# Pads at both ends of on-chip memory, dense operands at multiples of 512 bytes, and stored weight parts for one output chunk only

## The chip, the cores and the metric

One core of one Trainium2 chip. The metric is device time in microseconds (us), the median over runs of the whole program. Times of the kernel before: 3194.85, 3198.68 and 3200.09 us.

## What is computed

One hybrid decoder layer in fp32 on x of 1024 tokens by 2048 channels: a layer norm with shift and scale from a conditioning vector, one wide input projection, two mixers side by side (native sparse attention and a diagonal state-space layer with a GLU), their gated sum, an output projection and a second norm. Cut to what bears on the change:

```python
h = _ln(x) * (1.0 + scale[:, None, :]) + shift[:, None, :]
proj = h @ w_in[i]
...
m = jax.nn.sigmoid(ga) * (o_a @ w_branch_nsa[i]) + jax.nn.sigmoid(gb) * (o_b @ w_branch_ssm[i])
y = m @ w_out[i]
x = _ln(DEEPNORM_ALPHA * x + gate[:, None, :] * y) * ln_g[i] + ln_b[i]
```

All dense products run on TensorE with fp32 split into two parts: a value is cast to fp32r (`hi`), the rest is `lo`, and a product is hi·hi + hi·lo + lo·hi, three matmuls of 128x128 (stationary) by 128x512 (moving).

## The kernel before

The program is written in a tile framework: tiles come from pools, and a scheduler orders each engine's instructions by a priority (the program's order, with weight units raised by `WPRI`). All DMAs are issued by SyncE (SP) on one queue, in order.

**Input products** (`mm6`, L126, L127, L130). `w_unit` (L106) loads 128x512 of weights (`wraw`, L111), casts them on ScalarE (`whi`, L113) and takes the rest on VectorE (`wlo`, L115). The weights are the stationary operand, the normed input (`hhi`, `hlo`, 32 tiles in the pool `xh` on the right side of on-chip memory) is the moving one.

**Branch products** (`product`, L487 to L489). Weights are stationary again; the moving operand is `op`, from the pool `opd` on the left side or `opx` on the right (the second half of the tokens in `glu` and `branch_ssm`).

**Output projection** (`out_tokens`, L601; `times`, L617, matmuls L619 to L621). Here the roles are swapped: `m`, the merged branches, is stationary (pool `mp`, right side), and weights are moving. It runs twice, first for the tokens 512 to 1023, then (`final`) for 0 to 511. Each run goes over four chunks `c` of 512 output columns, each of 16 k's and 4 blocks of 128 tokens. In the first run the weights of chunks 0 and 3 are stored after the split, as parts, in DRAM (`wo_d`, stores at L633); the second run loads these parts (`wohi`, `wolo`, L628) instead of loading, casting and subtracting again. Chunks 1 and 2 are split anew in both runs. During chunk 3 of the first run the `m` of the second half is loaded (`mraw`, L558) and split (L560, L561). During chunk 0 of the second run the norms of the first run (`later`) are done: L611 on ScalarE, L612 and L613 on VectorE, stores to `out` at L614. In chunk 3 of the second run (`split_up`) the four blocks go in two pairs, and the parts of k = 8 to 15 are loaded ahead (`kept`) into `opd`; they are used after k = 0 to 7.

**Where the operands lie.** Left-hand pools are stacked upwards from the end of the constants' pool `cst`, right-hand pools downwards from the top. All dense tiles are multiples of 512 bytes per partition, so one offset holds for a whole side: in the built kernel before, the left pools begin at 416 modulo 512, the right ones at 480. Moving/stationary offsets are thus 480/416 for the input products, 416/416 for branch products with `opd` (480/416 with `opx`), and 416/480 for the output projection.

Of the kernel before, what the change touches and what calls it, by code (L numbers as in the profile page):

```python
# [5 lines left out]
F32 = mybir.dt.float32  # L6
# [11 lines left out]
KT = 16  # L18
# [7 lines left out]
PS_, PT, PWB, WR = 3, 2, 4, 2  # L26
MR = 2
EARLY = (6, 6, 6, 4)


def hybrid_kernel(tc, A, out):
# [19 lines left out]
def _hybrid(es, tc, A, out):  # L51
# [31 lines left out]
    bf_d = scratch("bf_d", [128, 512])  # L83
    ob_d = [[scratch(f"ob_d{hf}_{i}", [2, 128, 512]) for i in range(8)] for hf in range(2)]
    oa_d = [[scratch(f"oa_d{hf}_{g}", [2, 128, 2, 512]) for g in range(G)] for hf in range(2)]
    wo_d = {c: [[scratch(f"wo_d{c}_{k}_{i}", [128, 512]) for i in range(2)] for k in range(KT)] for c in (0, 3)}
    mb_d = [scratch(f"mb_d{i}", [128, 512]) for i in range(16)]

    cst = es.enter_context(tc.tile_pool(name="cst", bufs=1))
    ident = cst.tile([128, 128], F32, name="ident")  # L90
    ld(ident, A["ident"])
    ones = cst.tile([128, 128], F32, name="ones")
    V.memset(ones, 1.0)
    bada = cst.tile([128, KT, 2], F32, name="bada")
    ld(bada, A["bada"])
    mods = cst.tile([128, KT, 2], F32, name="mods")
    gts = cst.tile([128, NB, 48], F32, name="gts")

    wp = es.enter_context(tc.tile_pool(name="wp", bufs=3))
    stp = es.enter_context(tc.tile_pool(name="st", bufs=3))  # L100

# [43 lines left out]

    NS = 3
    units = []


    def load_wa(n):  # L150
# [204 lines left out]
    def gate_steps():  # L355

        for c in range(4):
            gp = bank()
            for hf in range(2):
                cs = slice(512 * c + 256 * hf, 512 * c + 256 * hf + 256)  # L360
                o = gp[:, 256 * hf:256 * hf + 256]
                for u in range(4):
                    wg = stp.tile([128, 4, 256], F32, name="wg", tag="stg")
                    ld(wg, A["w_gate"][4 * u:4 * u + 4, :, cs].rearrange("k p c -> p k c"))
                    for i in range(4):
                        r = 32 * i
                        PE.matmul(o[r:r + 32], cP[:, 4 * u + i], wg[:, i], start=u == 0, stop=u == 3, tile_position=(0, r))
                    yield
            cs = slice(512 * c, 512 * c + 512)
            s = stage()  # L370
            t, b = s[:, :512], s[0:32, 512:]
            S.copy(t, gp)
            S.copy(b, gp[0:32])
            ld(b, A["b_gate"][0:1, cs].to_broadcast([32, 512]))
            g2 = bank()
            PE.matmul(g2[0:32], ones[:, 0:32], t, start=True, stop=True)
            V.tensor_tensor(b, b, g2[0:32], op=ADD)
            st_(gate_d[:, cs], b[0:1])

# [80 lines left out]
    p1.close()  # L460


    hb = cst.tile([128, 8], F32, name="hb")
    ld(hb, A["b_glu"])
    V.tensor_scalar(hb, hb, 0.5, None, op0=MUL)

# [134 lines left out]
    def out_tokens(m, hf, final, ahead=None, later=iter(())):  # L601

        r, stt = [None] * 4, [None] * 4

        def norm(b, n=2):
            mv = row_stats(nc, tl, stt[b])
            nm = tl.tile([128, 1], F32, name="nm", tag="nm", bufs=2)
            V.tensor_scalar(nm, mv[:, 0:1], mv[:, 1:2], -1.0, op0=MUL, op1=MUL)
            for c in range(n):
                cs = slice(D // n * c, D // n * (c + 1))  # L610
                S.activation(r[b][:, cs], r[b][:, cs], AF.Identity, bias=nm, scale=mv[:, 1:2])  # L611
                V.tensor_tensor(r[b][:, cs], r[b][:, cs], rows["ln_g"][:, cs], op=MUL)  # L612
                V.tensor_tensor(r[b][:, cs], r[b][:, cs], rows["ln_b"][:, cs], op=ADD)  # L613
                ld(out[512 * hf + 128 * b:512 * hf + 128 * b + 128, cs], r[b][:, cs])  # L614
                yield

        def times(a, mk, b, hi, lo, k):  # L617
            t = slice(128 * b, 128 * b + 128)
            PE.matmul(a, mk[0][:, t], hi, start=k == 0, stop=False)  # L619
            PE.matmul(a, mk[0][:, t], lo, start=False, stop=False)  # L620
            PE.matmul(a, mk[1][:, t], hi, start=False, stop=k == KT - 1)  # L621

        def parts(c, k, pool=None):

            if final and c in wo_d:
                hl = [(pool or wp).tile([128, 512], F32R, name="wo" + n, tag="op" if pool else "w" + n) for n in ("hi", "lo")]
                for t, d in zip(hl, wo_d[c][k]):
                    rd(f(t), d)  # L628
            else:
                hl = w_unit(A["w_out"][k][:, 512 * c:512 * c + 512], [128, 512], tl)  # L630
                if c in wo_d:
                    for t, d in zip(hl, wo_d[c][k]):
                        st_(d, f(t))  # L633
            return hl

        for c in range(4):
            cs = slice(512 * c, 512 * c + 512)
            split_up = final and c == 3
            if ahead and c == 3:
                ahead()  # L640
            kept = {}
            if split_up:

                with tc.high_priority(offset=WPRI):
                    kept = {k: parts(c, k, opd) for k in range(8, KT)}
            for bs in ((0, 1), (2, 3)) if split_up else (range(4),):
                acc = [psum_a() if c % 2 and b > 1 else psum_e() for b in bs]
                for k in range(8 if split_up else KT):
                    with tc.high_priority(offset=WPRI):
                        hi, lo = parts(c, k)  # L650
                    for b, a in zip(bs, acc):
                        times(a, m[k], b, hi, lo, k)
                    if c == 0:
                        next(later, None)
                for b, a in zip(bs, acc):
                    for k in kept:
                        times(a, m[k], b, *kept[k], k)
                    x = fetch(A["x"][512 * hf + 128 * b:512 * hf + 128 * b + 128, cs])[:, :512]
                    S.mul(x, x, ALPHA)
                    if c == 0:  # L660
                        r[b] = tl.tile([128, D], F32, name="r", tag="r", bufs=5)
                        stt[b] = tl.tile([128, 4, 6], F32, name="stt", tag="stt", bufs=5)
                    with tc.high_priority(offset=WPRI if split_up else 0):
                        V.tensor_tensor(r[b][:, cs], a, rows["gate"][:, cs], op=MUL)
                        V.tensor_tensor(r[b][:, cs], r[b][:, cs], x, op=ADD)
                        V.bn_stats(stt[b][:, c], r[b][:, cs])
                    if split_up:
                        for _ in norm(b, 4 if b == 3 else 2):
                            pass
        return (None for b in range(4) for _ in norm(b, 4))  # L670
# [97 lines left out]
class Attention:  # L768
# [25 lines left out]
    def group(self, g):  # L794
        V, rd, NK = self.nc.vector, self.rd, self.NK
        self.g = g

        def f(ap):
            return ap.bitcast(F32)


        if self.first == 0:
            self.window_keys(0, NK)
        self.KS = self.tl("ks", [128, NK], F32R, "k")
        rd(f(self.KS), self.k_d[0][g].rearrange("i d t -> (i d) t")[:, :NK])

        self.BN = self.tl("bn", [128, 4, 256], F32, "kv")
        t = self.tz_d[g]
        rd(self.BN, bass.AP(tensor=t.tensor, offset=t.offset + 127, ap=[[383, 128], [384 * 128, 4], [1, 256]]))

        self.VC = self.tl("vc", [128, 2, 128], F32R, "kv")
        for e in range(2):
            V.memset(f(self.VC)[64 - 64 * e:128 - 64 * e, e], 0.0)
            rd(f(self.VC)[64 * e:64 * e + 64, e], self.vcc_d[:, g])
        if self.BF is None:
            self.BF = self.tl("bf", [128, 384])
            t = self.bf_d
            rd(self.BF, bass.AP(tensor=t.tensor, offset=t.offset + 127, ap=[[511, 128], [1, 384]]))
        nb = NK // 128
        self.VS = self.tl("vs", [128, nb, 128], F32R, "kv")  # L820
        self.VW = self.tl("vw", [128, nb, 128], F32R, "kv")
        for v, t in ((self.VW, self.v_d[1][g]), (self.VS, self.v_d[0][g])):
            for hf in range(2):
                c = slice(4 * hf, min(4 * hf + 4, nb))
                rd(f(v)[:, c], t[hf][:, :c.stop - c.start])
        self.BC = self.tl("bc", [128, 4, 120 - 8 * self.first], F32, "kv")
        V.memset(self.BC[:, :, 0:48], 0.0)
        V.memset(self.BC[:, :, 63:], NEG)
        V.tensor_copy(self.BC[:, :, 48:63], self.BN[:, :, 31:256:16])

    def window_keys(self, key0, n):

# [17 lines left out]
    def unit(self, qb):  # L850
# [37 lines left out]
        joint = key0 == 0  # L888

        def compressed(h, ps):  # L890
            b0 = 56 - 8 * qb
            m = reduce(0, h, [(ps, self.BC[:, h, b0:b0 + 64], pc[:, h])])
            S.activation(pc[:, h], pc[:, h], AF.Exp, bias=m, scale=-1.0, accum_out=sums[:, h, 0:1])

# [574 lines left out]
```

## Time and profile before

| | |
|---|---|
| runs, us | 3194.85, 3198.68, 3200.09 |
| profiled execution, us | 3197.64 |
| its span, us | 3195.9 |
| mean granted TensorE clock (share of 2.4 GHz) | 0.992 |
| TensorE busy | 97% of the span, 15573 instructions |
| VectorE, ScalarE busy | 51%, 35% |
| moved by DMA | 459.38 MB, mean 144 GB/s |

The profile is one execution. Busy shares say which engine is full over the whole span; windows of it say which one is full in a stretch. A matmul's time in the rows runs from its start to its last result; consecutive matmuls overlap, so the distance from start to start is shorter than that.

### The profile page before, as it was taken

The numbers are of one execution on the slowest core, as the hardware profiler recorded it, in microseconds if no ns is written. First come the engines' busy times: TensorE is split into PE (matmuls) and PEld (weight loads), VectorE is DVE, ScalarE is ACT, GpSimd is POOL, SyncE is SP. The second block draws the span as 40 slices with busy tenths as digits, with TensorE's granted clock in tenths as the row PEclk, the third lists the DMA queues.
The fourth block names the chain that finished last, engine by engine and source line by source line (L and its number), as shares of the span: only waits on it lengthen the run. The fifth ranks groups of instructions, "written<-read, shape, count | busy, mean of one in ns | idle before, by whom it ended". The sixth has DMA issues, their size and how long they took to land.

```text
span 3195.9 us, 43129 instructions
## 1 busy us (share of the span) xinstructions
PE 3113.6 (97%) x15573; PEld 2532.1 (79%) x15573; DVE 1632.5 (51%) x4593; ACT 1112.3 (35%) x2313; POOL 34.7 (1%) x36
## 2 busy tenths in 40 slices
PE   7999999999999999999999999999999999999896
PEld 3467788888888888888888888888888887888685
DVE  8445678753443334334433334427877665634535
ACT  4212222222443334333433334325654533323321
POOL 0000000000000000000000000000000000000000
PEclk9999999999999999999999999999999999999999
DMA  9764433344322232222322222246768445756835
GB/s 336 246 180 152 160 110 121 114 130 125 113 90 77 80 104 78 70 70 84 100 78 69 71 86 90 73 158 196 237 197 266 140 131 172 246 194 207 307 115 174
DMA packets 302221, 459.38 MB, mean 144 GB/s; under 512 B 42164, under 2 KB 141812, under 8 KB 302008
## 3 DMA queue, kind: packets, MB, share of 16 engines
q1 hardware_dynamic: 302008, 456.64, 44.7%
q8 instruction: 122, 2.00, 0.3%
q14 instruction: 91, 0.75, 0.1%
HBM read 345.09 MB, written 114.85 MB: 144 GB/s over the span
## 4 chain that ended last, share of the span: by engine, by line
PE 92%; DMA 6%; DVE 1%; SPq 1%; ACT 0%; issue 0%; DVEq 0%; ACTq 0%
PE dps L126 17%; PE dps L130 17%; PE dps L127 17%; PE po L989 4%; PE ps L846 4%; PE pt L967 4%; PE pa L487 3%; PE pa L489 3%; PE pa L488 3%; PE e L619 3%; PE e L620 3%; PE e L621 2%; PE mp L189 1%; DMA wohi<-wo_d 1%; PE pa L619 1%; PE pa L620 1%
## 5 line engine op out<-in xcount | busy, mean ns | idle before, releaser
L126 PE MATMUL dps<-hhi,whi 128*128 128x512 f32 x2336 | 927.3, 397 | 0.0
L127 PE MATMUL dps<-hlo,whi 128*128 128x512 f32 x2336 | 924.2, 396 | 0.0
L130 PE MATMUL dps<-hhi,wlo 128*128 128x512 f32 x2336 | 746.4, 396 | 0.0
L115 DVE TENSOR_TENSOR wlo<-wraw,whi 128x512 fp32r<-128x512 f32 x512 | 353.7, 691 | 632.2 <-ACT whi L113 614.6
L113 ACT CAST whi<-wraw 128x512 fp32r<-128x512 f32 x512 | 316.7, 619 | 997.2 <-PE dps L127 594.2
L126 PEld LDWEIGHTS dps<-hhi,whi 128*128 128x128 f32 x2336 | 440.1, 188 | 101.0 <-issue 9.0
L127 PEld LDWEIGHTS dps<-hlo,whi 128*128 128x128 f32 x2336 | 440.1, 188 | 90.3 <-issue 2.5
L130 PEld LDWEIGHTS dps<-hhi,wlo 128*128 128x128 f32 x2336 | 433.0, 188 | 89.5 <-issue 1.9
L972 DVE TENSOR_TENSOR ptl<-pt,pth 128x512 fp32r<-128x512 f32 (+1 forms) x320 | 196.7, 620 | 270.4 <-ACT pth L971 267.7
L971 ACT CAST pth<-pt 128x512 fp32r<-128x512 f32 (+1 forms) x320 | 166.3, 530 | 441.6 <-PE pt L967 440.3
L487 PE MATMUL pa<-op,whi 128*128 128x512 f32 x528 | 210.2, 400 | 5.5 <-ACT whi L113 3.2
L488 PE MATMUL pa<-op,whi 128*128 128x512 f32 x528 | 209.4, 397 | 2.4 <-DMA op<-oa_d 2.4
L489 PE MATMUL pa<-op,wlo 128*128 128x512 f32 x528 | 209.0, 397 | 0.0
L961 ACT ACTIVATE psl<-psl,mn 128x128 f32<-128x128 f32 (+7 forms) x128 | 99.1, 775 | 89.9 <-DVE mn L874 89.5
L487 PEld LDWEIGHTS pa<-op,whi 128*128 128x128 f32 x528 | 99.9, 189 | 25.8 <-ACT whi L113 4.0
L488 PEld LDWEIGHTS pa<-op,whi 128*128 128x128 f32 x528 | 99.9, 189 | 21.9 <-DMA op<-oa_d 2.8
L489 PEld LDWEIGHTS pa<-op,wlo 128*128 128x128 f32 x528 | 99.8, 189 | 20.0 <-DVE wlo L115 0.4
L620 PE MATMUL e<-wlo,m 128*128 128x512 f32 x288 | 114.4, 397 | 0.0
L621 PE MATMUL e<-whi,m 128*128 128x512 f32 x288 | 113.4, 394 | 0.0
L915 ACT ACTIVATE pw<-pw,mn 128x640 f32<-128x640 f32 (+4 forms) x128 | 88.8, 694 | 29.9 <-DVE mn L874 29.6
L619 PE MATMUL e<-whi,m 128*128 128x512 f32 x288 | 96.4, 396 | 0.0
L846 PE MATMUL ps<-ks,q 128*128 128x512 f32 (+3 forms) x384 | 96.0, 350 | 0.2 <-DVE mn L874 0.2
(306 smaller groups left out, 4223.2 us busy)
## 6 DMA issues: line engine op xcount, KB each, us to landing
wraw<-in_w_in SPq DMA_DIRECT2D x304, 256.0 KB, 3.1
wa<-in_w_ss SPq DMA_DIRECT2D x64, 512.0 KB, 5.3
wraw<-in_w_out SPq DMA_DIRECT2D x96, 256.0 KB, 3.4
wg<-in_w_gate SPq DMA_DIRECT2D x32, 512.0 KB, 3.7
q<-q_d SPq DMA_DIRECT2D x64, 256.0 KB, 4.1
wraw<-in_w_bn SPq DMA_DIRECT2D x64, 256.0 KB, 3.5
wohi<-wo_d SPq DMA_DIRECT2D x40, 256.0 KB, 5.2
wolo<-wo_d SPq DMA_DIRECT2D x40, 256.0 KB, 5.1
```

Of the source, the lines that this page charges most:

```text
L113: S.copy(hi, raw)
L115: V.tensor_tensor(lo, raw, f(hi), op=SUB)
L126: PE.matmul(ps[hf], hi[:, ku], hhi[k][:, c], start=a, stop=False)
L127: PE.matmul(ps[hf], hi[:, ku], hlo[k][:, c], start=False, stop=False)
L130: PE.matmul(ps[hf], lo[:, ku], hhi[k][:, c], start=False, stop=z)
L487: PE.matmul(ps, hi[:, j], x[k][0], start=k == 0, stop=False)
L488: PE.matmul(ps, hi[:, j], x[k][1], start=False, stop=False)
L489: PE.matmul(ps, lo[:, j], x[k][0], start=False, stop=k == 7)
L619: PE.matmul(a, mk[0][:, t], hi, start=k == 0, stop=False)
L620: PE.matmul(a, mk[0][:, t], lo, start=False, stop=False)
L846: PE.matmul(ps[:, :z - a], q[:, 4 * i + h], K[:, c0 + a:c0 + z], start=i == 0, stop=i == 1)
L972: V.tensor_tensor(lo[0:n, :w], tp[0:n, :w], f(hi[0:n, :w]), op=SUB)
```

## The change

**Pads.** Two tiles that nobody uses are put at the ends: 224 bytes per partition behind the constants, 480 at the right-hand top. With smaller constants (`ones` 32 columns in place of 128, `bada` and `mods` moved into a pool that is closed early, `hb` allocated with the constants) the left pools of the built kernel begin at 18944 = 37 x 512 bytes, the right ones end at 228864 = 447 x 512. All operands of the three kinds of dense product are then at 0 modulo 512, moving and stationary. The attention's tiles, which differ in size, shift too, to offsets that are not 0 (early part: `ks` from 0 to 96, `q` from 384 to 224).

**Stored parts.** `wo_d` is there for chunk 3 only. The first run stores 32 pieces of 256 KB less, and chunk 0 of the second run goes through `w_unit`: 16 loads of 256 KB, 16 casts and 16 subtractions, in place of 32 loads.

**Chunk 3 of the second run.** The kept parts come between the others: after k = 1, 3, 5, 7 the kept 8, 9, 10, 11, and 12 to 15 at the end.

```diff
+PAD_LEFT, PAD_RIGHT = 224, 480
...
-    wo_d = {c: [[scratch(f"wo_d{c}_{k}_{i}", [128, 512]) for i in range(2)] for k in range(KT)] for c in (0, 3)}
+    wo_d = {c: [[scratch(f"wo_d{c}_{k}_{i}", [128, 512]) for i in range(2)] for k in range(KT)] for c in (3,)}
...
-    ones = cst.tile([128, 128], F32, name="ones")
+    ones = cst.tile([128, 32], F32, name="ones")
     V.memset(ones, 1.0)
-    bada = cst.tile([128, KT, 2], F32, name="bada")
-    ld(bada, A["bada"])
-    mods = cst.tile([128, KT, 2], F32, name="mods")
     gts = cst.tile([128, NB, 48], F32, name="gts")
 
+    hb = cst.tile([128, 8], F32, name="hb")
+
+    cst.tile([128, PAD_LEFT // 4], F32, name="pad")
+    es.enter_context(tc.tile_pool(name="padr", bufs=1, side="right")).tile([128, PAD_RIGHT // 4], F32, name="padr")
...
                     for b, a in zip(bs, acc):
                         times(a, m[k], b, hi, lo, k)
+                    if split_up and k % 2:
+                        for b, a in zip(bs, acc):
+                            times(a, m[8 + k // 2], b, *kept[8 + k // 2], 8 + k // 2)
                     if c == 0:
                         next(later, None)
                 for b, a in zip(bs, acc):
-                    for k in kept:
+                    for k in range(12, KT) if split_up else ():
                         times(a, m[k], b, *kept[k], k)
...
-        self.BC = self.tl("bc", [128, 4, 120 - 8 * self.first], F32, "kv")
...
+        self.bc0 = c = 64 - 8 * self.end
+        self.BC = self.tl("bc", [128, 4, 120 - 8 * self.first - c], F32, "kv")
```

The last piece makes a bias tile of the attention as small as the blocks in use. Lines of the changed file are up to 8 higher (L628 becomes L632, L619 to L621 become L623 to L625, L611 L615).

How the order moves, at three places. SyncE's queue where the second run of the output projection begins, in the kernel before (`wo_d_0_0_226` is the hi part of chunk 0's k = 0, `wo_d_13_0_284` that of chunk 3's k = 13, `mraw` a raw `m`):

```order
L628 DMA wohi<-wo_d_0_0_226 128x512
L628 DMA wohi<-wo_d_13_0_284 128x512
L628 DMA wolo<-wo_d_0_1_227 128x512
L628 DMA wolo<-wo_d_13_1_285 128x512
L496 DMA stg<-in_x 128x512 x2
L628 DMA wohi<-wo_d_1_0_228 128x512
L628 DMA wohi<-wo_d_14_0_286 128x512
L628 DMA wolo<-wo_d_1_1_229 128x512
L558 DMA mraw<-m_d_190 128x512
```

and now:

```order
L632 DMA wohi<-wo_d_13_0_252 128x512
L632 DMA wolo<-wo_d_13_1_253 128x512
L500 DMA stg<-in_x 128x512 x2
L632 DMA wohi<-wo_d_14_0_254 128x512
L113 DMA wraw<-in_w_out 128x512
L632 DMA wolo<-wo_d_14_1_255 128x512
L500 DMA stg<-in_x 128x512
L562 DMA mraw<-m_d_190 128x512
```

Two loads of parts for each k of chunk 0 have become one load of raw weights, and the loads of kept parts (k = 13, 14) stay between them.

ScalarE in the same place, now (`L564` splits `m`, `L615` is a norm's activation, `L115` the new cast of weights):

```order
L115 CAST whi<-wraw 128x512
L615 ACTIVATE r<-r,nm,mv 128x512 x4
L564 ACTIVATE m<-mraw 128x512
L615 ACTIVATE r<-r,nm,mv 128x512 x4
L666 ACTIVATE stg<-stg 128x512 x2
L115 CAST whi<-wraw 128x512
```

In the kernel before there was no cast there, and the norms stood eight in a row (`L611 ACTIVATE ... x8`). The casts now stand between the norms, behind up to four activations at a time.

TensorE in chunk 3 of the second run, second accumulator of the first pair left out: the kernel before goes from k = 6 and 7 (`m_26392`, `m_26398`) to the kept k = 8 (`m_26404`) and 9 only at the end.

```order
L619 MATMUL e_27864<-wohi_27926,m_26392 128x512
...
L619 MATMUL e_27864<-wohi_27936,m_26398 128x512
...
L619 MATMUL e_27864<-wohi_27832,m_26404 128x512
...
L619 MATMUL e_27864<-wohi_27836,m_26410 128x512
```

Now (k = 0, 1, then the kept 8, then 2, 3, then the kept 9; `wohi_27805` and `wohi_27809` are kept ones):

```order
L623 MATMUL e_27837<-wohi_27839,m_26297 128x512
...
L623 MATMUL e_27837<-wohi_27849,m_26303 128x512
...
L623 MATMUL e_27837<-wohi_27805,m_26345 128x512
...
L623 MATMUL e_27837<-wohi_27865,m_26309 128x512
...
L623 MATMUL e_27837<-wohi_27875,m_26315 128x512
...
L623 MATMUL e_27837<-wohi_27809,m_26351 128x512
```

Between two loaded k's and the next two there is now a k whose parts have been in memory for long.

## Rows read from the trace of the kernel before

**Rows 1.** The page: busy time, the granted clock in 40 slices, the chain that ended last.
```profile
PE 3113.6 (97%) x15573; PEld 2532.1 (79%) x15573; DVE 1632.5 (51%) x4593; ACT 1112.3 (35%) x2313; POOL 34.7 (1%) x36
...
PEclk9999999999999999999999999999999999999999
...
PE 92%; DMA 6%; DVE 1%; SPq 1%; ACT 0%; issue 0%; DVEq 0%; ACTq 0%
...
PE dps L126 17%; PE dps L130 17%; PE dps L127 17%; PE po L989 4%; PE ps L846 4%; PE pt L967 4%; PE pa L487 3%; PE pa L489 3%; PE pa L488 3%; PE e L619 3%; PE e L620 3%; PE e L621 2%; PE mp L189 1%; DMA wohi<-wo_d 1%; PE pa L619 1%; PE pa L6
```

**Rows 2.** Groups of instructions by line, engine PE: busy us and mean ns, then idle us.
```profile
L126 PE MATMUL dps<-hhi,whi 128*128 128x512 f32 x2336 | 927.3, 397 | 0.0
...
L487 PE MATMUL pa<-op,whi 128*128 128x512 f32 x528 | 210.2, 400 | 5.5 <-ACT whi L113 3.2 <-DMA op<-ob_d 1.9 <-DMA op<-oa_d 0.4
...
L487 PE MATMUL e<-op,whi 128*128 128x512 f32 x112 | 44.8, 400 | 3.1 <-DVE pth L1063 1.8 <-ACT whi L113 1.2
```

**Rows 3.** Windows: us, then busy (xcount) of PE, PEld, DVE, ACT, POOL; clock, DMA, GB/s.
```profile
690.00:740.00 50.00, 50.00 (x220) 41.00 (x220) 17.14 (x25) 11.66 (x18) 0.00 (x0) 1.00 0.70 166
2725.00:2775.00 50.00, 50.00 (x222) 41.41 (x221) 29.70 (x47) 17.07 (x28) 0.00 (x0) 1.00 0.75 246
2850.00:2900.00 50.00, 50.00 (x216) 40.30 (x215) 19.10 (x30) 13.60 (x22) 0.00 (x0) 1.00 0.36 115
```

**Rows 4.** Waits of engine PE: total us, times, longest us.
```profile
PE e L619 <- DMA wohi<-wo_d: 18.7, 12, 9.4
...
PE pa L619 <- DMA wohi<-wo_d: 2.4, 3, 1.4
...
PE pa L620 <- DMA wolo<-wo_d: 0.5, 1, 0.5
```

**Rows 5.** Timeline of PE, second half's chunk 0: start, us, line, [idle before, releaser].
```profile
2968.95 0.39 PE L621 MATMUL pa<-whi,m 128*128 128x512 f32 x1
...
2978.71 2.08 PE L619 MATMUL e<-wohi,m 128*128 128x512 f32 x4 [9.37 <-DMA wohi<-wo_d]
...
2981.14 0.63 PE L621 MATMUL e<-wohi,m 128*128 128x512 f32 x1
...
2981.57 0.63 PE L620 MATMUL e<-wolo,m 128*128 128x512 f32 x1
...
2993.11 0.50 PE L619 MATMUL e<-wohi,m 128*128 128x512 f32 x1 [1.75 <-DMA wohi<-wo_d]
...
3001.32 0.50 PE L619 MATMUL e<-wohi,m 128*128 128x512 f32 x1 [2.35 <-DMA wohi<-wo_d]
...
3034.05 0.63 PE L619 MATMUL e<-whi,m 128*128 128x512 f32 x2
```

**Rows 6.** Windows as in rows 3: chunk 0 of the second half, and the handover.
```profile
2969.00:3034.00 65.00, 49.42 (x194) 36.65 (x193) 35.37 (x82) 20.58 (x33) 0.00 (x0) 0.92 0.83 295
2950.00:3000.00 50.00, 36.78 (x143) 27.20 (x142) 37.59 (x84) 24.29 (x39) 0.00 (x0) 0.90 1.03 372
```

**Rows 7.** DMA issues from 2950 to 3010 us: count, KB each, median us to landing.
```profile
wohi<-wo_d SPq DMA_DIRECT2D x18, 256.0 KB, 5.5
...
out<-r SPq DMA_DIRECT2D x16, 256.0 KB, 5.3
...
mraw<-m_d SPq DMA_DIRECT2D x9, 256.0 KB, 5.6
```

**Rows 8.** The page's groups of instructions: the weight split on ACT and DVE.
```profile
L115 DVE TENSOR_TENSOR wlo<-wraw,whi 128x512 fp32r<-128x512 f32 x512 | 353.7, 691 | 632.2 <-ACT whi L113 614.6
L113 ACT CAST whi<-wraw 128x512 fp32r<-128x512 f32 x512 | 316.7, 619 | 997.2 <-PE dps L127 594.2
```

**Rows 9.** Groups by line from 2969 to 3016 us, engine ACT.
```profile
L611 ACT ACTIVATE r<-r,nm,mv 128x512 f32<-128x512 f32 x16 | 11.5, 801 | 0.8 <-DVE nm L608 0.8
```

**Rows 10.** Timeline of PE in chunk 3 of the second half.
```profile
3130.76 0.50 PE L619 MATMUL e<-wohi,m 128*128 128x512 f32 x1 [2.13 <-DMA wohi<-wo_d]
...
3136.84 0.50 PE L619 MATMUL e<-wohi,m 128*128 128x512 f32 x1 [0.80 <-DMA wohi<-wo_d]
```

More of the change, by code (lines that the diff above doesn't have):

```diff
@@ L147, in _hybrid @@
     units = []
+    bada = p0.tile([128, KT, 2], F32, name="bada")
+    ld(bada, A["bada"])
+    mods = p0.tile([128, KT, 2], F32, name="mods")
     def load_wa(n):
@@ L375, in gate_steps @@
             g2 = bank()
-            PE.matmul(g2[0:32], ones[:, 0:32], t, start=True, stop=True)
+            PE.matmul(g2[0:32], ones, t, start=True, stop=True)
             V.tensor_tensor(b, b, g2[0:32], op=ADD)
@@ L460, in _hybrid @@
     p1.close()
-    hb = cst.tile([128, 8], F32, name="hb")
     ld(hb, A["b_glu"])
@@ L825, in group @@
                 rd(f(v)[:, c], t[hf][:, :c.stop - c.start])
-        self.BC = self.tl("bc", [128, 4, 120 - 8 * self.first], F32, "kv")
-        V.memset(self.BC[:, :, 0:48], 0.0)
-        V.memset(self.BC[:, :, 63:], NEG)
-        V.tensor_copy(self.BC[:, :, 48:63], self.BN[:, :, 31:256:16])
+        self.bc0 = c = 64 - 8 * self.end
+        self.BC = self.tl("bc", [128, 4, 120 - 8 * self.first - c], F32, "kv")
+        V.memset(self.BC[:, :, 0:48 - c], 0.0)
+        V.memset(self.BC[:, :, 63 - c:], NEG)
+        V.tensor_copy(self.BC[:, :, 48 - c:63 - c], self.BN[:, :, 31:256:16])
     def window_keys(self, key0, n):
@@ L890, in compressed @@
         def compressed(h, ps):
-            b0 = 56 - 8 * qb
+            b0 = 56 - 8 * qb - self.bc0
             m = reduce(0, h, [(ps, self.BC[:, h, b0:b0 + 64], pc[:, h])])
```

## Prediction

> **What bounds the kernel now.** I read the page from the top. TensorE is busy for 3113.6 of 3195.9 us, on the chain of waits it holds 92% and DMA 6%, and the granted clock is at its upper level (2.4 GHz) in nearly every slice [rows 1]. VectorE and ScalarE are far from full. So two things can shorten the program: less time for each matmul, or less idle time of TensorE. The groups by line give the counts: 3 x 2336 = 7008 matmuls of the input products (L126, L127, L130), 3 x (528 + 112) = 1920 of the branch products (L487 to L489) [rows 2], and, by the loops, 16 k x 4 chunks x 4 blocks x 2 halves x 3 = 1536 of the output projection. All are 128x512.
>
> The mean of one instruction is no price here, since it overlaps the next one. The price is the distance from start to start, which comes out of windows in which TensorE does nothing but one kind of product. Three such windows of 50 us [rows 3] hold 220 matmuls (input products), 222 (branch products) and 216 (output projection). A window also counts a matmul that only reaches over its edge; one lasts 0.39 us, so about 1.7 of the count are extra. That leaves 218.3, 220.3 and 214.3, and the **pitches are 229.0, 227.0 and 233.3 ns**. Three kinds of product with the same shape, type and clock, and with little other work, differ by up to 6.3 ns. Busy shares of the other engines don't order them: the branch window has the most DVE, ACT and DMA work of the three and the shortest pitch. What does differ is where the operands start, modulo 512 bytes (moving/stationary): 480/416, 416/416, 416/480.
>
> The second reading is TensorE's list of waits [rows 4]: 18.7 us before L619 for loads of stored weight parts, 2.4 and 0.5 us more on the `pa` banks. The timeline [rows 5] puts half of the 18.7 at one place: the first half's last matmul starts at 2968.95, the next one only at 2978.71, and by then the clock has fallen to the lower level: the starts at 2981.14 and 2981.57 are 0.43 us apart.
>
> **The change part by part.**
>
> *Pads.* All dense operands go to offset 0/0. No row has that pair. What the rows do show is that the pair with equal offsets is the fastest (227.0), a moving operand 64 bytes ahead costs 2.0 ns more, and 64 bytes behind 6.3 more. I take the price of 0/0 from the row it resembles most, the equal pair: 227.0 for all. Input products: 7008 x 2.0 = 14.0 us. Branch products: those whose operands sit in the right-hand pool, the second half in glu (8 x 24) and in the SSM branch (16 x 24), are 576 at 480/416; by the input row's price they gain 576 x 2.0 = 1.2 us; the other 1344 are at equal offsets already and gain nothing. Output projection: 1536 x 6.3 = 9.7 us. Sum **25 us**, all of it on TensorE, which sets the end.
> Bounds: the low clock shows what the array needs if data is always there. 0.43 us at half the clock [rows 5] is 0.215 at the full one, so no offset can bring a pitch below about 215 ns. Then the gain would be 7008 x 14 + 1344 x 12 + 576 x 14 + 1536 x 18.3 = 98 + 16 + 8 + 28 = 150 us. The other end is the worst row, 233.3: 7008 x 4.3 + 576 x 4.3 + 1344 x 6.3 = 30 + 2.5 + 8.5 = 41 us lost.
> The attention's operands change offsets too, but to other odd ones (keys 0 to 96 in the early part, for instance). On the chain its scores (L846) and values (L989) have 4% each [rows 1], some 256 us; 6.3 ns in 230 either way would be 2.7% of that, 7 us at most; I take 0.
>
> *Chunk 0 of the second half: split again instead of loaded.* From 2969.2 to 3034 us this chunk takes 64.9 us for 192 matmuls; at 233.3 ns they need 44.8. The excess of 20.1 us is idle time (9.4 + 1.8 + 2.4 = 13.5 in the three longest waits [rows 5]), smaller waits and matmuls at the lower clock. The queue is the reason: DMA is busy 83% over those 65 us [rows 6], and from 2950 to 3010 the stretch moves 36 loads of stored parts, 16 stores of `out`, 9 of `mraw` and more, each about 5.5 us from issue to landing [rows 7]. The change takes 32 loads of 256 KB out and puts 16 in, 4 MB less, and issues no store of those parts in the first half (32 of 256 KB; TensorE's list of waits names no load of that stretch, so I count nothing for them).
> What it adds: 16 casts on ACT and 16 subtractions on DVE, 16 x 0.62 = 9.9 and 16 x 0.69 = 11.1 us [rows 8]. Beside what DVE and ACT do now in the stretch (35.4 and 20.6 us [rows 6]) that makes 46.5 and 30.5 us. **DVE thus becomes the floor of this stretch**: 46.5 us, just over the 192 x 0.227 = 43.6 that TensorE needs. ACT has a trap of its own: a norm is four activations of 0.80 us in a row [rows 9], a cast queued behind them is up to 3.2 us late, and three buffers of weights cover about 3 x 12 x 0.227 = 8 us. So casts hide, subtractions nearly. I take 52 us: the floor, 2 to 3 us for the `m` splits that still wait for `mraw`, and 2 to 3 us of lower clock. Gain of this stretch 64.9 - 52 = 13; of that 192 x 6.3 = 1.2 us were in the pads' sum already, so **12 us**. Bounds: DVE full without a gap, 18; all of the old excess replaced by waits for DVE, 0.
>
> *Chunk 3 interleaved.* For each pair of blocks eight k's are loaded during use, 16 x 256 KB = 4.2 MB for 8 x 6 x 0.233 = 11.2 us of matmuls. That is 374 GB/s, what a full stretch here reaches (372 GB/s [rows 6]), and TensorE catches up with the loads: waits of 2.13 and 0.80 us in the first pair [rows 10], up to 1.4 in the second [rows 4]. Afterwards eight kept parts run without any load. With one kept part after every second loaded one, the same bytes have 12 x 6 x 0.233 = 16.8 us, 250 GB/s. The waits on `pa` (2.4 + 0.5) and these two on `e` (2.13 + 0.80) make 5.8 us, and each is followed by some starts that are further apart. I take **5 us**, since the first loads of a pair may still be late; bounds 0 and 8.
>
> Kept parts are now read earlier and free their buffers no earlier for anyone; nothing is queued behind them. The smaller `BC` and `ones` tiles, and moving `bada`, `mods` and `hb`, change a few instructions of under a microsecond and cost nothing on the chain.
>
> Sum: 25 + 12 + 5 = 42 us. The profiled execution took 3197.6 us; 3197.6 - 42 = 3155.6, say **3155 us**. The runs' median is 3198.68, about 1 us more, so the sum holds for it too. Forecast's own range, with the tail between 5 and 26 us and 0/0 a little better or worse than the equal pair: 3135 to 3172.
>
> **The rivals.**
>
> *A. Offset 0/0 removes the stall altogether* (12%). The mechanism: what holds the pitch above 215 is that rows of an operand start off a boundary, and only then is the operand fetched in more pieces. For: the low-clock starts show the array itself is not the limit, and none of the three pairs is on a multiple of 512. Against: the equal pair, as badly aligned as the others, already is best, and its rest of 12 ns need not come from alignment. Price 150 + 17 us: 3030 us. Half of it (pitch 221) gives 7008 x 8 + 1344 x 6 + 576 x 8 + 1536 x 12.3 = 88, with the tail 3092 us; I count that half-way case with the forecast's side. The Trainium skill, TensorE: Matmul & The Clock Gate, section Back-to-back issue gap, gives 512/2.4 + 2.5 = 215.8 ns for one isolated gap; by it this rival is the normal state, but no window of the kernel before reaches it.
>
> *B. Offsets are not the cause* (16%). The windows differ in more than offsets: the input products alternate two banks with one stationary operand, the output projection takes a new stationary block in every matmul. If that makes the pitches, the pads give nothing, and only the tail is left: 3197.6 - 17 = 3180 us (3172 to 3192). Against: branch and output products both change the stationary operand from matmul to matmul and still differ by 6.3 ns. The Trainium skill speaks for B: SBUF — State Buffer, section A bandwidth-pool intuition that's wrong, says TensorE's weight loads have a second, independent read port, so that the two operands should not disturb each other. The trace leaves that open, because no pair of windows there differs in offsets alone.
>
> *C. Slower: 0/0 is a bad pair* (10%). If moving and stationary rows that start at the same boundary collide, the pitch goes to that of the worst row, 233.3 ns, on all products: +41 us, less the tail's 17: 3197.6 + 24 = 3222 us (3205 to 3240). It decides from a mean pitch 17 / 10,464 = 1.6 ns above today's. For: two of three pairs are worse than the best, and no row has 0/0. Against: equal offsets are the best row.
>
> *D. The handover turns from a DMA wait into a DVE wait, with no gain in pitch* (4%). If DVE, at its 46.5 us floor, serves norms ahead of the weight splits, TensorE waits as long as now: about 3193 to 3200 us.
>
> **How the numbers follow.** Forecast with the half-way case 58%, A 12%, B 16%, C 10%, D 4%. About 0.2% (6 us) is what a measurement of this kernel can tell from no change. Faster by more: the forecast, A, and 13 of B's 16, 83%. Within: the rest of B and most of D, 6%. Slower: C and a remnant of D, 11%. The range runs from the half-way case to the top of B: **3088 to 3195**; left out are A and most of C and D.
>
> **What would show it.** The three windows should hold about 222 matmuls in 50 us each; 220 and 216 again would be B, 234 would be A, 216 everywhere C. In the handover the wait of 9.37 us should be gone, no wait above 3 us in its place, and chunk 0 should take 50 to 54 us with DVE nearly full. The list of waits should have `wohi` below 3 us. If the pitch is right but the sum is not, the tail or the attention was mis-sized; if the handover shows long waits for `wlo`, D's step is what I got wrong.

## The result, and the profile after

The changed kernel takes 3167.4 us (median; 3165.0 to 3170.6) against 3199.0: ratio 0.9904, 95% interval 0.9887 to 0.9921, so 1.0% faster. The forecast was 3155 us (range 3088 to 3195). The profiled execution's span went from 3195.9 to 3163.9 us, 32 us less where 42 were expected.

The page's busy times and chain, which answer to [rows 1]:

```profile
PE 3089.1 (98%) x15573; PEld 2531.0 (80%) x15573; DVE 1640.3 (52%) x4609; ACT 1122.6 (35%) x2329; POOL 35.5 (1%) x36
...
PE 92%; DMA 3%; DVE 2%; ACT 1%; issue 1%; SPq 1%; DVEq 0%; ACTq 0%
```

Windows of pure products, as in [rows 3], and chunk 0 of the second half, as in [rows 6] (columns: us, PE, PEld, DVE, ACT, POOL busy with counts; granted clock, DMA share, GB/s):

```profile
690.00:740.00 50.00, 50.00 (x223) 41.38 (x222) 17.15 (x26) 11.98 (x19) 0.00 (x0) 1.00 0.67 157
2725.00:2775.00 50.00, 50.00 (x223) 41.39 (x221) 29.72 (x47) 17.89 (x29) 0.00 (x0) 1.00 0.59 196
2850.00:2900.00 50.00, 50.00 (x222) 41.40 (x221) 20.04 (x31) 13.40 (x22) 0.00 (x0) 1.00 0.38 119
...
2948.00:3011.00 63.00, 51.19 (x196) 38.90 (x195) 45.83 (x98) 29.45 (x50) 0.00 (x0) 0.89 0.70 239
```

All three products now have the count of the best one before: 220, 222 and 216 became 223, 223 and 222, a pitch (distance from start to start) of 226 to 227 ns. In chunk 0 the clock is not full (0.89), as before (0.92). TensorE's waits, which answer to [rows 4]:

```profile
PE e L623 <- ACT whi L115: 7.9, 6, 4.7
PE e L624 <- DVE wlo L117: 4.3, 4, 2.1
...
PE e L623 <- DMA wohi<-wo_d: 1.5, 1, 1.5
PE pa L623 <- DMA wohi<-wo_d: 1.4, 1, 1.4
```

The waits for stored parts have shrunk from 21.1 to 2.9 us, but waits for ScalarE's cast and VectorE's subtraction, 12.2 us, have come in their place. The timeline of chunk 0, as in [rows 5]:

```profile
2947.90 0.39 PE L625 MATMUL pa<-whi,m 128*128 128x512 f32 x1
2949.09 1.20 PE L623 MATMUL e<-whi,m 128*128 128x512 f32 x4 [0.80 <-ACT whi L115]
...
2965.50 2.07 PE L623 MATMUL e<-whi,m 128*128 128x512 f32 x4 [4.69 <-ACT whi L115]
...
2985.36 0.49 PE L624 MATMUL e<-wlo,m 128*128 128x512 f32 x1 [2.10 <-DVE wlo L117]
...
3010.70 0.61 PE L623 MATMUL e<-whi,m 128*128 128x512 f32 x2
```

The long wait at the handover is gone (9.37 to 0.80 us), but one of 4.69 us has come a little later. Counted from one pitch (0.2 us) after the last start of the first half to the first start of chunk 1, the stretch goes from 2948.1 to 3010.7: 62.6 us, where it was 64.9.

The table reads the same points from the timeline of every kernel (us; "chunk 0" with the wait ahead of it; "end" from the last matmul's start to the end of the span). Runs of one block shared a chip, with the kernel before beside them: 3193.6 us beside e1, e2, e3 and e5, 3194.5 beside e0, e4, e6 and e8, and 3192.8 beside e9, e11, e12 and e13. Ratios compare across blocks better than times.

| kernel | ratio to before (95%) | chunk 0 | chunk 1 | chunk 3 | end |
|---|---|---|---|---|---|
| before | 1 | 64.9 | 44.8 | 54.1 | 18.2 |
| changed | 0.9904 (0.9887 to 0.9921) | 62.6 | 43.5 | 46.8 | 19.4 |
| e1_equal_odd | 0.9935 (0.9918 to 0.9951) | 62.2 | 43.5 | 50.9 | 19.3 |
| e2_right_256 | 0.9926 (0.9911 to 0.9941) | 61.7 | 43.5 | 46.7 | 19.3 |
| e3_left_only | 1.0056 (1.0041 to 1.0071) | 62.2 | 44.8 | 48.1 | 19.3 |
| e5_no_pads | 0.9987 (0.9977 to 0.9996) | 63.4 | 44.8 | 48.2 | 19.3 |
| e0_changed_again | 0.9915 (0.9900 to 0.9930) | 61.5 | 43.5 | 46.9 | 19.4 |
| e4_pads_alone | 0.9939 (0.9922 to 0.9955) | 66.1 | 43.5 | 53.6 | 18.1 |
| e6_stored_chunk0 | 0.9921 (0.9904 to 0.9937) | 62.8 | 43.5 | 46.9 | 19.3 |
| e8_norm_pool | 0.9951 (0.9933 to 0.9969) | 72.0 | 43.5 | 47.2 | 19.5 |
| e9_right_128 | 1.0040 (1.0025 to 1.0055) | 62.1 | 44.6 | 50.6 | 19.4 |
| e11_kept_late | 0.9902 (0.9887 to 0.9917) | 52.9 | 43.9 | 49.3 | 19.4 |
| e12_norm_dve | 0.9890 (0.9875 to 0.9905) | 53.7 | 43.5 | 47.6 | 17.5 |
| e13_both | 0.9872 (0.9856 to 0.9889) | 44.5 | 43.5 | 47.3 | 17.8 |

### The profile page after: what moved, and what is told of

Read it like the earlier page. It is cut to its first block, busy times and chain, and to the rows that moved or that the text cites. A ratio compares the mean times of both kernels' runs of the same rounds, so it can differ in the third digit from the quotient of the medians.

```text
span 3163.9 us, 43079 instructions
## 1 busy us (share of the span) xinstructions
PE 3089.1 (98%) x15573; PEld 2531.0 (80%) x15573; DVE 1640.3 (52%) x4609; ACT 1122.6 (35%) x2329; POOL 35.5 (1%) x36
## 4 chain that ended last, share of the span: by engine, by line
PE 92%; DMA 3%; DVE 2%; ACT 1%; issue 1%; SPq 1%; DVEq 0%; ACTq 0%
PE dps L128 17%; PE dps L132 17%; PE dps L129 17%; PE po L997 4%; PE ps L854 4%; PE pt L975 4%; PE pa L493 4%; PE pa L492 4%; PE pa L491 4%; PE e L624 2%; PE e L623 2%; PE e L625 2%; PE mp L194 1%; PE e L493 1%; PE e L492 1%; PE e L491 1%
## 5 line engine op out<-in xcount | busy, mean ns | idle before, releaser
L117 DVE TENSOR_TENSOR wlo<-wraw,whi 128x512 fp32r<-128x512 f32 x528 | 364.4, 690 | 617.2 <-ACT whi L115 599.0
L115 ACT CAST whi<-wraw 128x512 fp32r<-128x512 f32 x528 | 326.8, 620 | 990.0 <-PE dps L129 585.0
L624 PE MATMUL e<-wlo,m 128*128 128x512 f32 x352 | 138.9, 395 | 4.3 <-DVE wlo L117 4.3
L625 PE MATMUL e<-whi,m 128*128 128x512 f32 x352 | 138.4, 393 | 0.0
L623 PE MATMUL e<-whi,m 128*128 128x512 f32 x352 | 117.2, 398 | 8.0 <-ACT whi L115 7.9
```

The lines of the kernel that those rows point to most:

```text
L115: S.copy(hi, raw)
L117: V.tensor_tensor(lo, raw, f(hi), op=SUB)
```

## Experiments on the offsets

My theory was that equal offsets of moving and stationary operand make the short pitch. Each kernel is the changed one with other pads; the order of the work is that of the changed kernel.

**e1**, all operands at 416: `PAD_LEFT, PAD_RIGHT = 128, 64`.

> The changed kernel with smaller pads (128 and 64 bytes): every dense operand at 416 modulo 512, moving and stationary alike, so equal offsets but no multiple of 64. Theory (equal offsets make the short pitch): as the changed kernel, 3162 to 3172 us, and 222 to 223 matmuls in each of the 50 us windows of input products, branch products and output projection. Rival (the multiple of 512 itself counts): the input products and the output projection keep most of their old pitch, 220 and 216 per window, and the time is some 15 to 20 us longer, about 3185.

**e2**, left 0, right 256: `PAD_LEFT, PAD_RIGHT = 224, 224`.

> The changed kernel with 224 bytes of pad on the right: left at 0, right at 256, so input products at 256/0 and the output projection at 0/256; order of the work unchanged. Theory (equal offsets): both get longer than 226.7 ns, by something between the 2 and the 7 ns of the kernel before, 3180 to 3200 us. Rival 1 (multiples of 64 bytes are enough; before, all were 32 past one): as the changed kernel, 3162 to 3172. Rival 2 (a multiple of 512 for each): only the operand on the right is off, about half of the loss, 3172 to 3182.

**e3**, left 0, right 480: the line of `padr` is taken out.

> The changed kernel with the left pad alone: left at 0, right at 480, so input products at 480/0 and the output projection at 0/480. Theory (equal offsets): the distance is 32 bytes, so both stay longer than 226.7 ns, windows of 215 to 221, 3175 to 3195 us. Rival (each operand's own boundary): the side that is aligned has its gain, so either the input products or the output projection reaches 222 per window and the other does not.

**e9**, left 0, right 128: `PAD_LEFT, PAD_RIGHT = 224, 352`.

> The changed kernel with 352 bytes of pad on the right: input products at 128/0, output projection at 0/128. Theory (the pitch is short when the two offsets agree modulo 256, and long otherwise): over 226.7 ns for both, 216 to 221 matmuls per window, 3180 to 3210 us. Rival (agreeing modulo 128 is enough): as the changed kernel, 222 per window, 3164 to 3172 us.

Windows, for each kernel input products first, then the output projection. e1:

```profile
690.00:740.00 50.00, 50.00 (x222) 41.43 (x221) 17.11 (x26) 11.99 (x19) 0.00 (x0) 1.00 0.67 159
2840.00:2890.00 50.00, 50.00 (x223) 41.39 (x222) 20.06 (x31) 13.42 (x23) 0.00 (x0) 1.00 0.35 117
```

e2:

```profile
690.00:740.00 50.00, 50.00 (x222) 41.42 (x221) 17.28 (x27) 11.98 (x19) 0.00 (x0) 1.00 0.69 165
2840.00:2890.00 50.00, 50.00 (x223) 41.40 (x222) 19.37 (x30) 13.50 (x23) 0.00 (x0) 1.00 0.36 118
```

e3 (other windows, so that each holds one kind of product only):

```profile
700.00:750.00 50.00, 50.00 (x216) 40.26 (x215) 17.40 (x26) 12.06 (x19) 0.00 (x0) 1.00 0.66 156
2840.00:2890.00 50.00, 50.00 (x216) 40.14 (x215) 18.97 (x31) 13.52 (x22) 0.00 (x0) 1.00 0.35 115
```

e9:

```profile
695.00:745.00 50.00, 50.00 (x216) 40.52 (x216) 17.26 (x26) 11.96 (x19) 0.00 (x0) 1.00 0.66 155
2840.00:2890.00 50.00, 50.00 (x217) 40.55 (x216) 20.08 (x32) 13.58 (x22) 0.00 (x0) 1.00 0.36 116
```

416/416 is as fast as 0/0, so a multiple of 512 is not what counts. 256/0 and 0/256 are fast too, against my theory as I put it and in line with e2's rival 1; but that rival falls with e9, since 128 is a multiple of 64 and both 128/0 and 0/128 are slow. A left pad alone is slow too: e3 took 3211.4 us where I expected 3175 to 3195, and is 0.6% behind the kernel before. What fits all ten pairs seen: **the pitch is short (222 to 223 per window) when the two offsets agree modulo 256, and 2 to 7 ns longer otherwise** (216 to 220, with 480/416 the mildest). It is a matter of the two operands to each other, not of either one alone. The distances tried are 0 and 256, which are fast, and 32, 64 and 128, which are slow; others were not tried, and no run shows by what mechanism the distance acts.

With equal windows, e1 and e2 took 3173.4 and 3170.2 us, a ratio of 0.9935 and 0.9926 where the changed kernel has 0.9904 and (as e0) 0.9915: chunk 3 of e1 is 4 us longer (a wait of 3.2 us for `wohi`), and the stretch of late attention and branch products is 2 to 3 us longer in both.

## Experiments on the tail

**e5**, offsets of the kernel before (left pad 128 bytes, no right pad), so the tail's two edits alone.

> The changed kernel with the offsets of the kernel before (left 416, right 480), so only the change of stored parts and of chunk 3's order is left. Theory: the pads are worth 18 to 22 us, and this runs at 3185 to 3190; 220 and 216 matmuls per window as before; chunk 0 of the second half takes 62 to 65 us as before and only chunk 3 is shorter, about 48 us for 192 matmuls. Rival (the pads gave little, the tail and the late attention most): 3172 or less.

It came to 0.9987, 3190.1 us, with the old counts in the windows (input products, then the output projection):

```profile
690.00:740.00 50.00, 50.00 (x220) 41.00 (x220) 17.17 (x25) 12.04 (x19) 0.00 (x0) 1.00 0.69 166
2850.00:2900.00 50.00, 50.00 (x216) 40.30 (x215) 19.37 (x30) 13.60 (x22) 0.00 (x0) 1.00 0.34 115
```

Chunk 0 took 63.4 us, chunk 3 48.2. So of the tail's two edits the order of chunk 3 saves 5.9 us and the new split of chunk 0 only 1.5. After the last matmul 1.1 us are lost again; that comes with chunk 3's new order, since the end is 19.3 in e6, which keeps it, and 18.1 in e4, which doesn't.

**e0**, the changed kernel beside e4, e6 and e8.

> The changed kernel once more, as the base for the three beside it on the same chip: 0.990 to 0.992 of the time before.

It came to 0.9915, 3167.0 us.

**e4**, pads alone: `wo_d` for `(0, 3)` again, and `for k in kept` at the end, without the interleaved lines.

> Pads as in the changed kernel; parts of chunks 0 and 3 stored, and kept parts used at the end, as before. Theory (the pads carry about three quarters, stored parts of chunk 0 nothing, chunk 3's order 6 us): 5 to 7 us over the changed kernel; the handover waits about 9 us for loads again and chunk 0 takes, with that wait, 61 to 65 us; chunk 3 takes 52 to 53 us. Rival (the rows of before carry over: splitting chunk 0 again saves 12 us): 17 us over the changed kernel.

3174.4 against 3167.0 us for e0: 7 us more, about as expected; chunk 3 took 53.6 us, chunk 0 66.1. Against the kernel before on the same chip (3194.5) the pads alone thus save 20 us.

**e6**, only `wo_d` for `(0, 3)` again.

> The changed kernel, but chunk 0's parts are stored and loaded again as before. Theory (waiting for DVE has taken the place of waiting for the queue): within 3 us of the changed kernel, chunk 0 with the wait ahead of it 61 to 65 us, DVE with more idle time in it. Rival: 12 us longer.

3168.8 against 3167.0, the same within the runs; chunk 0 62.8 against 61.5 us. TensorE waits for loads instead:

```profile
PE e L623 <- DMA wohi<-wo_d: 14.7, 5, 8.7
```

Splitting chunk 0 again thus is worth 1 to 2 us, not 12.

**e8**, sixteen additions moved off VectorE.

```diff
-                V.tensor_tensor(r[b][:, cs], r[b][:, cs], rows["ln_b"][:, cs], op=ADD)
+                (V if final else P).tensor_tensor(r[b][:, cs], r[b][:, cs], rows["ln_b"][:, cs], op=ADD)
```

> The changed kernel, with the 16 additions of ln_b in the first half's norms on GpSimd instead of VectorE: 16 x 0.68 = 10.9 us off VectorE in chunk 0 of the second half. Theory (DVE is what this chunk waits for): chunk 0 gets 5 to 10 us shorter, from 62.6 to 53 to 58, and so does the program. Rival 1 (the raw m come late over the queue): no change, within 2 us. Rival 2 (GpSimd slows DVE or is much slower itself): chunk 0 longer.

Chunk 0 got 10 us longer (72.0 against 61.5 in e0), which is rival 2. The groups of that stretch in e8, GpSimd and then VectorE:

```profile
L617 POOL TENSOR_TENSOR r<-r,ln_b 128x512 f32<-128x512 f32 x16 | 26.9, 1714 | 318.9 <-DMA wraw<-in_w_out 313.0 <-DVE r L616 5.3 <-DVE rsd L44 0.6
```

```profile
L616 DVE TENSOR_TENSOR r<-r,ln_g 128x512 f32<-128x512 f32 x16 | 21.0, 1343 | 0.2
...
L565 DVE SCALAR_TENSOR_TENSOR m<-mraw,m 128x512 fp32r<-128x512 f32 x7 | 7.8, 1113 | 0.4 <-ACT m L564 0.4
```

The same two groups in chunk 0 of the changed kernel:

```profile
L616 DVE TENSOR_TENSOR r<-r,ln_g 128x512 f32<-128x512 f32 x16 | 10.6, 684 | 0.2
...
L565 DVE SCALAR_TENSOR_TENSOR m<-mraw,m 128x512 fp32r<-128x512 f32 x6 | 4.0, 675 | 0.0
```

VectorE's operations beside GpSimd's take 1343 and 1113 ns as a mean in place of 684 and 675, so nothing was taken off VectorE, and the test doesn't decide about the floor. The timeline of e8 holds four of GpSimd's additions in a row (first fence); VectorE from 2970.9 us on, while they run, is in the second:

```profile
2967.58 6.73 POOL L617 TENSOR_TENSOR r<-r,ln_b 128x512 f32<-128x512 f32 x4 [0.63 <-DVE rsd L44]
```

```profile
2969.77 1.75 DVE L616 TENSOR_TENSOR r<-r,ln_g 128x512 f32<-128x512 f32 x1
2971.44 1.75 DVE L672 TENSOR_TENSOR r<-r,stg 128x512 f32<-128x512 f32 x1
2973.22 0.69 DVE L673 BATCH_NORM_STATS2 stt<-r 128x6 f32<-128x512 f32 x1
```

The operations that read two tiles take 1.75 us there, the one that reads a single tile 0.69. The Trainium skill, SBUF — State Buffer, section Who interferes with whom, says that a VectorE instruction with two inputs in on-chip memory contends with a GpSimd instruction that reads there, and that one with a single input does not, outside VectorE's two-port modes. The trace agrees in these rows.

**e11**, kept loads after chunk 0.

```diff
                 for t, d in zip(hl, wo_d[c][k]):
+                    if pool:
+                        V.tensor_copy(t[:, 0:1], r[3][:, 0:1])
                     rd(f(t), d)
...
-            kept = {}
-            if split_up:
-
-                with tc.high_priority(offset=WPRI):
-                    kept = {k: parts(c, k, opd) for k in range(8, KT)}
+            if final and c == 2:
+                kept = {k: parts(3, k, opd) for k in range(8, KT)}
```

> The changed kernel, with the 16 loads of kept parts held back until chunk 0 of the second half is done (each tile is first touched by a one-column copy that needs that chunk's result): 4.2 MB less on the queue in the handover, the same in sum. Theory (VectorE sets the length of chunk 0): at most 3 us shorter, with DVE as full as before. Rival (loads over the full queue set it): raw weights and raw m land in 3 instead of 5 us and chunk 0 is 5 to 10 us shorter.

**e12**, norms without ScalarE (`nm` goes too).

```diff
-                S.activation(r[b][:, cs], r[b][:, cs], AF.Identity, bias=nm, scale=mv[:, 1:2])
-                V.tensor_tensor(r[b][:, cs], r[b][:, cs], rows["ln_g"][:, cs], op=MUL)
-                V.tensor_tensor(r[b][:, cs], r[b][:, cs], rows["ln_b"][:, cs], op=ADD)
+                V.scalar_tensor_tensor(r[b][:, cs], r[b][:, cs], mv[:, 0:1], rows["ln_g"][:, cs], op0=SUB, op1=MUL)
+                V.scalar_tensor_tensor(r[b][:, cs], r[b][:, cs], mv[:, 1:2], rows["ln_b"][:, cs], op0=MUL, op1=ADD)
```

> The changed kernel, with each norm as two operations on VectorE, (r - mean) * ln_g and * rstd + ln_b, in place of one activation on ScalarE and two on VectorE: 16 x 0.80 = 12.8 us off ScalarE in chunk 0, nothing off VectorE. Theory (casts queued behind a norm's four activations are the waits for whi, 7.9 us): these waits go, chunk 0 is 3 to 6 us shorter, and the end after the last matmul 1 to 3 us. Rival (VectorE alone sets the length): chunk 0 changes by less than 1.5 us.

**e13**, both.

> Both edits together (kept parts late, norms without ScalarE). Theory: if queue, ScalarE and VectorE share the waiting in chunk 0, the two add up, 8 to 12 us less than the changed kernel. Rival (VectorE is the floor): no more than the better one of the two alone.

Chunk 0 fell to 52.9, 53.7 and, with both, 44.5 us. Against the two profiles of the changed kernel (62.6 and, as e0, 61.5) each edit takes 8 to 10 us and both together 17 to 18, so they add up. The mean granted clock of the stretch rises with it, from 0.89 to 0.94 in e11 and e12 and to 1.00 in e13. The three largest waits of any engine in chunk 0 of the changed kernel:

```profile
ACT whi L115 <- PE e L625: 17.2, 8, 2.5
DVE wlo L117 <- ACT whi L115: 16.6, 10, 2.4
ACT whi L115 <- DMA wraw<-in_w_out: 11.9, 4, 5.2
```

VectorE, the supposed floor, stood idle 16.6 us there, waiting for casts. ScalarE waited 11.9 us for raw weights on the full queue; its 17.2 us for `L625` are waits for a weight buffer that TensorE still reads, so there the casts were ahead. ScalarE's timeline at the start of the chunk shows both reasons for late casts:

```profile
2948.42 0.62 ACT L115 CAST whi<-wraw 128x512 fp32r<-128x512 f32 x1 [2.66 <-DMA wraw<-in_w_out]
...
2952.95 0.62 ACT L115 CAST whi<-wraw 128x512 fp32r<-128x512 f32 x1 [2.69 <-DMA wraw<-in_w_out]
...
2957.11 0.62 ACT L115 CAST whi<-wraw 128x512 fp32r<-128x512 f32 x1 [1.35 <-DMA wraw<-in_w_out]
2957.63 2.93 ACT L615 ACTIVATE r<-r,nm,mv 128x512 f32<-128x512 f32 x4
2960.47 0.61 ACT L564 ACTIVATE m<-mraw 128x512 fp32r<-128x512 f32 x1
2960.99 2.92 ACT L615 ACTIVATE r<-r,nm,mv 128x512 f32<-128x512 f32 x4
2963.80 1.14 ACT L666 ACTIVATE stg<-stg 128x512 f32<-128x512 f32 x2
2964.84 0.60 ACT L115 CAST whi<-wraw 128x512 fp32r<-128x512 f32 x1
```

The first casts each wait for their raw weights. Then eight norm activations, a split of `m` and two of `stg` stand between one cast and the next for 7.2 us, and that next cast is the one that TensorE waits 4.69 us for. The window of chunk 0 in e13, and VectorE's longest groups in it:

```profile
2946.00:2991.00 45.00, 44.57 (x195) 36.25 (x195) 43.76 (x90) 16.71 (x31) 0.00 (x0) 1.00 0.72 237
```

```profile
L117 DVE TENSOR_TENSOR wlo<-wraw,whi 128x512 fp32r<-128x512 f32 x17 | 11.3, 677 | 0.2 <-ACT whi L115 0.2
L613 DVE SCALAR_TENSOR_TENSOR r<-r,mv,ln_g 128x512 f32<-128x512 f32 x16 | 11.0, 746 | 0.0
L614 DVE SCALAR_TENSOR_TENSOR r<-r,mv,ln_b 128x512 f32<-128x512 f32 x16 | 10.9, 745 | 0.0
```

VectorE is busy 43.8 of 45 us, with the wait for `whi` down to 0.2, and the clock stays at its upper level. Here VectorE is full, and so is TensorE, whose 192 matmuls need 43.5 us; which of the two would bind is not shown. My theory for e11 (at most 3 us) fell: with the loads of the kept parts out of the way, about half of the excess of chunk 0 is gone, as its rival had it. But raw weights did not land faster after their issue (a median of 3.3 us in chunk 0 of the changed kernel, 3.7 in e11), and ScalarE still waited 9.4 us for them, so how that edit helps is shown only in part. e12 took more off chunk 0 than the 3 to 6 us expected, and 1.9 us off the end. In e11 the program gains less than chunk 0: its ratio is 0.9902, its chunk 3 is 2.5 us longer, with a wait of 2.3 us for `wohi`, and the changed kernel was not run on that chip. e13 is the best kernel of the study, 3150.3 us, 1.3% under the one before.

## Why the prediction was right and wrong

- **The pitch at 0/0: right.** 227.0 ns was taken from the equal pair, and all three windows show it. Rival A (alignment removes the stall) and rival C (0/0 collides) fell with the counts of 222 to 223, and B with e5: offsets alone move 220 and 216 to 222 and more. That the two operands should not disturb each other, which B drew from the second, independent read port for weight loads in the Trainium skill, SBUF — State Buffer, section A bandwidth-pool intuition that's wrong, does not hold for these products: e2 against e9 shows that shifting one operand by 128 bytes costs some 6 ns a matmul. Whether the read ports have to do with it, no run shows.
- **Input products, 14 us expected, 10 measured** (from their first matmul to their last the time went from 2090.4 to 2080.4 us): the term was mis-sized. I multiplied a pure window's difference by all matmuls (7008 of them; there are 7296, since [rows 2] leaves out 288 that write `acc`). Beside attention and state-space pieces it is smaller, because each piece is followed by several longer starts in either kernel. The changed kernel's timeline after one such piece (starts of every sixth matmul):

```profile
1512.57 0.48 PE L854 MATMUL ps<-ks,q 128*128 128x256 f32 x2
...
1513.14 0.40 PE L128 MATMUL dps<-hhi,whi 128*128 128x512 f32 x1
...
1514.54 0.40 PE L128 MATMUL dps<-hhi,whi 128*128 128x512 f32 x1
...
1515.92 0.39 PE L128 MATMUL dps<-hhi,whi 128*128 128x512 f32 x1
...
1517.29 0.39 PE L128 MATMUL dps<-hhi,whi 128*128 128x512 f32 x1
```

  Six matmuls take 1.40, 1.38 and 1.37 us, that is 233, 230 and 228 ns each. Over all places where input products follow other work, the mean distances (those between 200 and 260 ns) are:

| step after the other work | before, ns | changed, ns | steps before |
|---|---|---|---|
| 1 and 2 | 232.3 | 232.1 | 706 |
| 3 to 6 | 230.2 | 230.2 | 1326 |
| 7 to 12 | 229.2 | 228.2 | 1564 |
| from 13 on | 229.1 | 226.7 | 2823 |

  The pitch only settles at 227 after about twelve. The first six steps, a third of all, gain nothing; the others make some 8 of the 10 us.
- **Output projection, 9.7 us expected: right.** Chunks 1 and 2 went from 44.8 to 43.5 us each, 6.7 ns a matmul; on 1536 that would be 10 us. Some 9 are in the program's time, since the last chunk of the first half gained only 0.2 us (44.6 to 44.4).
- **Branch products and late attention, 1 us expected, 6.3 measured** (from there to the output projection's first matmul: 644.2 to 637.9 us). e5, with the same order and the old offsets, took 645.1, so it comes with the pads. Pitch gives some 1.6 us of it; the rest lies in many short gaps and a few longer waits and was not settled: e2 had 640.6. So the pads' sum of 25 us, about what these stretches add up to (e4, by whole programs, gives 20, with an interval of 14 to 25), came out by luck: 4 us too many in the input products and 5 too few here cancel.
- **Chunk 0, 12 us expected, 1 measured** (2.3 less the pitch's 1.3). The step that failed is "So casts hide, subtractions nearly. I take 52 us". I summed VectorE's work, 46.5 us, and took that floor as reached but for 5 us. The sum was right (45.8 in the changed kernel, 43.8 in e13), but VectorE could not be kept fed. Raw weights came late (ScalarE waited 11.9 us for them) while the queue still carried the kept parts, and the casts stood behind norm activations, once for 7.2 us where I had reckoned with 3.2. Taking away the one (e11) or the other (e12) gives back 8 to 10 us each. That is rival D's outcome, a DMA wait turned into a wait on the split, but by another mechanism than D named: VectorE was idle, not full. Of the signs I had named, the windows and the loads of `wohi` (2.9 us of waits) held; chunk 0 of 50 to 54 us, no wait above 3 us and a nearly full VectorE did not.
- **Chunk 3, 5 us expected, 6 measured** (54.1 to 46.8, less 1.3 of pitch). Right.
- The end after the last matmul grew by 1.2 us, which I had not looked at.

The parts add up: 10.0 + 6.3 + 4.1 (first half's projection) + 2.3 + 2.6 (chunks 1 and 2) + 7.3 - 1.2 = 31.4 of the 32.0 us; most of the rest, 0.7, lies ahead of the first input product (55.4 to 54.7 us).

## What to carry to other kernels

Where TensorE streams one kind of product without a pause, count matmuls in equal windows per operand pair before asking for anything else: here a few ns of pitch, which follow from where two tiles start to each other, were worth 20 us (e4), the loads taken out of chunk 0 only 1 to 2 (e6), and one pad alone made the kernel slower (e3). An engine's summed work in a stretch is reached as a floor only if every input comes in time; look at what stands ahead of its feeder in each in-order queue. When a load moves from one queue to compute, take away what else crowds that moment (e11, e12) before counting the gain.

## What was not expected of the hardware

- The short pitch needs agreement modulo 256 bytes, not 512, and no alignment of either operand: 416/416, 0/0, 256/0 and 0/256 give 222 to 223 matmuls in 50 us; 128/0, 0/128, 480/0, 0/480 and 416/480 give 216 to 217; 480/416 gives 220.
- After other work the pitch of the input products takes about twelve matmuls to settle at 227 ns; the first six cost the same at 480/416 and at 0/0 (232 to 230 ns).
- VectorE operations with two inputs beside GpSimd's additions took 1.6 to 2 times as long in the mean (684 to 1343 ns, 675 to 1113). GpSimd's own additions took 1714 ns there, beside VectorE's 684 without GpSimd; what they take without VectorE beside them was not measured.
